# A decoder step whose first two token blocks enter the first projection without their norm

## Chip, cores and metric

One core of a Trainium2 chip. The metric is the device time of one execution in microseconds. Times inside an execution are counted from the start of the span, which runs from the first to the last instruction of the profiled execution.

## What is computed

One layer of a decoder that has two groups of heads: gated linear recurrence (HGRN2) and forgetting attention (FoX). 1024 prompt tokens and 8 x 4 sample tokens, 1024 wide, are normed, projected once, mixed by the two groups, gated, projected back and normed again. The places that matter here:

```python
def rmsnorm(x, w):
    y = xf * lax.rsqrt(jnp.mean(xf * xf, axis=-1, keepdims=True) + NORM_EPS)
    return (y * w.astype(jnp.float32)).astype(x.dtype)

hp = rmsnorm(xp, norm_w[l])
proj = jnp.einsum('btd,dc->btc', h, w_in_l)     # 4104 columns, split among the groups
hq, hf, hi, hgate, fq, fk, fv, ff, fgate = jnp.split(proj, offs, axis=-1)
```

The norm is a factor for each token times a weight for each column. The factor of a token can be taken out of the product: it scales one row of the projection.

## The kernel before

The 1024 prompt tokens are eight blocks of 128 (`tb` 0 to 7), the 32 sample tokens a ninth. A block lies transposed in SBUF, as eight chunks `k` of 128 model columns by 128 tokens (`xts[tb]`). A product of full precision is made of three passes of float32r: a value is split into a rounded part `hi` and the rest `lo`, and `hi*hi`, `hi*lo` and `lo*hi` are summed in PSUM. So all of x is kept as `xhi` and `xlo`, and each weight group as `hi` and `lo`.

The order of the work is written out by hand: every engine runs its instructions in program order, and all DMAs are issued from SP, in order.

- The norm of a block: ScalarE squares it, GpSimd multiplies it by the norm weight `nwT` (L245), VectorE reduces the squares (L249), TensorE sums them over the partitions with a matrix of ones (`norm_r`, in float32, which makes two instructions of one call), ScalarE makes the reciprocal root in two steps (`rstd`, L218 and L219), VectorE multiplies (L265), ScalarE rounds to `xhi` (L269), VectorE subtracts to `xlo` (L273).
- The first projection (`w1`, 512 columns, the recurrence's values): the weights come in four pairs of chunks. `split` makes `hi` (L308 on ScalarE or L310 on VectorE) and `lo` (L311 on VectorE or GpSimd). `proj` takes the block as the stationary side and makes three products of 512 columns for each k. Blocks 0 and 1 use the PSUM tiles `pa` and `pb`; blocks 2 to 7 follow in a loop, with the norm of the coming block between their products. `norm_r(2)` stands in the middle of block 1, `norm_r(3)` after k = 2 of block 2.
- `warm` issues products of ones with ones ahead of the first real work.
- The second projection (`w2`, 520 columns, the gates): `gate_group(tb)` makes two halves of 260 columns, each of 24 products in one of the two PSUM banks `pj`, and VectorE evacuates them (L488, L491, L492). Behind it `silu_mul` runs `Abs`, `Exp`, `Ln` on ScalarE (L336 to L338), one operation on VectorE (L339), `Exp` on ScalarE (L340) and two multiplies on GpSimd (L341, L343). `lower_bound` gives three small steps on `lb` to groups 3 to 5. `slab_split` prepares the first weight slab of the third projection (L448 on ScalarE, L449 on VectorE) after group 2.
- Then come the slabs (`slab`: weights stationary, x moving, all 1056 tokens), the recurrence, the attention, the sample tokens and the output projection. They read `xhi` and `xlo` of all blocks.

`U(i)` names SBUF slot i; a slot is used again when its readers are done. The loads of x wait for their slots, and those queued behind them on SP wait too.

Of the kernel before, what the change touches and what calls it, by code (L numbers as in the profile page):

```python
# [9 lines left out]
F32 = mybir.dt.float32  # L10
# [3 lines left out]
AF = mybir.ActivationFunctionType  # L14
OP = mybir.AluOpType
AX = mybir.AxisListType
# [4 lines left out]
D = 1024  # L21
NB = 8
KB = 8
# [47 lines left out]
def tile_hymba(ctx, tc, x_prompt, x_sample, x_b, x_d, cache_k_t, cache_v, cache_logf_t, state_hgrn, page_table,  # L71
# [10 lines left out]
    V, A, G, PE, SP = nc.vector, nc.scalar, nc.gpsimd, nc.tensor, nc.sync  # L82
# [8 lines left out]
    def f32(ap):  # L91
        return ap.bitcast(F32)

    def mm(out, lhsT, rhs, start, stop):
        PE.matmul(out, lhsT, rhs, start=start, stop=stop, skip_group_check=True)  # L95
# [6 lines left out]
    cst = ctx.enter_context(tc.tile_pool(name="cst", bufs=1))  # L102
# [6 lines left out]
    def U(i, n=TA, dt=F32, a=None):  # L109


        if i not in slots or slots[i].dtype != dt:
            slots[i] = wo["p"].tile([128, 1024], dt, name=f"u{i}") if i >= 100 else up.tile([128, TA], dt, name=f"u{i}")
        t = slots[i][:, :n]
        return t if a is None else t.rearrange("p (a b) -> p a b", a=a)

    def bank(name, n):
        if name not in banks:
            banks[name] = [0, [psum.tile([128, 512], F32, name=f"{name}{i}") for i in range(n)]]
        b = banks[name]  # L120
        b[0] += 1
        return b[1][b[0] % n]

    def ps_pj():
        return bank("pj", 2)

    def ps_s():
        return bank("ps", 3)
# [55 lines left out]
    nwT = cst.tile([128, KB], F32, name="nwT")  # L184
    xts = {}

    def load_x(tb):
        n = 128 if tb < NB else ND
        xts[tb] = U((17, 18, 24, 25, 26, 27)[tb % 6], D, a=KB)[:, :, :n]
        SP.dma_start(xts[tb], (x_b[tb] if tb < NB else x_d).rearrange("p (k t) -> p k t", k=KB))  # L190

    cc = cst.tile([128, K_MK], F32, name="cc")
# [5 lines left out]
    xhi = xp_.tile([128, KB, TA], F32R, name="xhi")  # L198
    xlo = xp_.tile([128, KB, TA], F32R, name="xlo")
# [13 lines left out]
    v = [U(20 + i, 1024, a=2) for i in range(4)]  # L213
# [3 lines left out]
    def rstd(r, ss, n):  # L217
        A.activation(r, ss, AF.Ln, bias=eps[:r.shape[0]], scale=1.0 / n)  # L218
        A.activation(r, r, AF.Exp, scale=-0.5)  # L219


    ones = wk[:, 384:512]
# [5 lines left out]
    def warm(n):  # L228
        for _ in range(n):
            mm(pw[:, :128], ones, ones, True, True)  # L230

    warm(11)

    ss_ = {}

    def norm_sq(tb, parts=1):
        xt, n = xts[tb], xts[tb].shape[-1]
        sq = U(15 + tb % 2, D, a=KB)[:, :, :n]
        o = 512 * (tb % 2)
        s = ss_[tb] = wk[:, o:o + 128 * parts].rearrange("p (a t) -> p a t", a=parts)[:, :, :n]  # L240
        for a in range(parts):
            k = slice(KB // parts * a, KB // parts * (a + 1))
            A.activation(sq[:, k], xt[:, k], AF.Square)
        for k in (slice(0, 4), slice(4, 8)):
            G.tensor_mul(xt[:, k], xt[:, k], nwT[:, k, None].to_broadcast([128, 4, n]))  # L245

        def reduce(a):
            k = slice(KB // parts * a, KB // parts * (a + 1))
            V.tensor_reduce(s[:, a], sq[:, k].rearrange("p k t -> p t k"), axis=AX.X, op=OP.add)  # L249

        return reduce

    def norm_r(tb):
        s, n = ss_[tb], xts[tb].shape[-1]
        p = ps_s()[:, :n]
        m = s.shape[1]
        for a in range(m):
            mm(p, ones, s[:, a], a == 0, a == m - 1)
        o = 512 * (tb % 2) + 256
        rstd(wk[:, o:o + n], p, D)  # L260

    def norm_mul(tb, k):
        xt, n = xts[tb], xts[tb].shape[-1]
        r = wk[:, 512 * (tb % 2) + 256:512 * (tb % 2) + 256 + n]
        V.tensor_mul(xt[:, k], xt[:, k], r[:, None, :].to_broadcast([128, k.stop - k.start, n]))  # L265

    def norm_hi(tb, k):
        xt, n, t0 = xts[tb], xts[tb].shape[-1], tb * 128
        A.activation(xhi[:, k, t0:t0 + n], xt[:, k], AF.Copy)  # L269

    def norm_lo(tb, k):
        xt, n, t0 = xts[tb], xts[tb].shape[-1], tb * 128
        V.tensor_sub(xlo[:, k, t0:t0 + n], xt[:, k], f32(xhi[:, k, t0:t0 + n]))  # L273

    halves = (slice(0, 4), slice(4, 8))

    def norm_a(tb):
        norm_sq(tb)(0)

    def norm_b(tb):  # L280
        norm_r(tb)
        for f in (norm_mul, norm_hi, norm_lo):
            for k in halves:
                f(tb, k)
        if tb == NB:
            V.tensor_copy(xd[:, :, :ND], f32(xhi[:, :, T:]))
            V.tensor_copy(xd[:, :, ND:], f32(xlo[:, :, T:]))
# [57 lines left out]
    w1 = Group(w_1, range(8), (12, 13, 14, 28))  # L345
    w2 = Group(w_2, (8, 9, 10, 11, 28, 29, 4, 5), (13, 14, 12, 13))
    every = slice(0, 512)
    load_x(0)
    SP.dma_start(nwT, norm_w.rearrange("o (k p) -> p (o k)", p=128))
    w1.load(0)  # L350
    load_x(1)
    w1.load(1)
    w1.load(2)
    w1.load(3)
    load_x(2)
    load_x(3)
    red = norm_sq(0, 2)
    red(0)
    red(1)
    w1.split(0, (V, V), (G, G))  # L360
    norm_r(0)
    warm(8)
    red = norm_sq(1)
    thirds = (slice(0, 2), slice(2, 4), slice(4, 8))
    for k in thirds:
        norm_mul(0, k)
        norm_hi(0, k)
    norm_lo(0, thirds[0])
    red(0)
    norm_lo(0, thirds[1])  # L370
    norm_lo(0, thirds[2])
    w1.split(1, (A, A), (V, V))
    load_x(4)
    load_x(5)
    SP.dma_start(cc, consts[:, :K_MK])
    pa, pb = ps_pj(), ps_pj()
    w1.proj(pa, 0, every, (0, 1))
    norm_r(1)
    w1.split(2)
    w1.proj(pa, 0, every, (2, 3))  # L380
    for f in (norm_mul, norm_hi, norm_lo):
        for k in halves:
            f(1, k)
    w1.split(3)
    w1.proj(pa, 0, every, (4, 5))
    red = norm_sq(2)
    w1.proj(pa, 0, every, (6, 7))
    A.activation(v[0][:, 0], pa, AF.Copy)
    red(0)
    w2.load(0)  # L390
    w2.load(1)
    w1.proj(pb, 1, every, (0, 1, 2, 3))
    norm_b(2)
    norm_a(3)
    load_x(6)
    w1.proj(pb, 1, every, (4, 5, 6, 7))
    A.activation(v[0][:, 1], pb, AF.Copy)
    load_x(7)
    load_x(8)
    w2.load(2)  # L400
    SP.dma_start(bf, bcast_row(b_fox_f, FH))
    SP.dma_start(hw, bcast_row(hg_norm_w, HK))
    for tb in range(2, NB):
        if tb < 6:
            norm_a(tb + 2)
        if tb == 7:
            w1.proj_d(vd, every)
        ps = ps_pj()
        w1.proj(ps, tb, every, range(3))
        if tb == 6:  # L410
            norm_b(NB)
        if tb < 7:
            norm_b(tb + 1)
        if tb == 5:
            norm_a(NB)
        w1.proj(ps, tb, every, range(3, 6))
        if tb < 5:
            w2.split(tb - 2)
        if tb == 3:
            w2.load(3)  # L420
        if tb == 7:
            w2.split(3)
        w1.proj(ps, tb, every, range(6, KB))
        A.activation(v[tb // 2][:, tb % 2], ps, AF.Copy)

    mk = U(17, 448, a=7)
    SP.dma_start(mk, consts[:, K_MK:K_N].rearrange("p (l b) -> p l b", l=7))

    v3 = cst.tile([96, 512], F32R, name="v3")
# [13 lines left out]
    def slab_split(i, half):  # L443
        if i < len(slabs):
            raw = U(12, 1024, a=KB)
            h, l = parts[i] = U(13 + i % 2, 1024, F32R, a=KB), U(15 + i % 2, 1024, F32R, a=KB)
            k = slice(4 * half, 4 * half + 4)
            A.activation(h[:, k], raw[:, k], AF.Copy)  # L448
            (V if i < 11 else G).tensor_sub(l[:, k], raw[:, k], f32(h[:, k]))  # L449
# [34 lines left out]
    def gate_group(tb):  # L484
        x = sg[tb // 2][:, tb % 2]
        ps = ps_pj()
        w2.proj(ps[:, :260], tb, slice(0, 260))
        V.tensor_copy(x[:, :260], ps[:, :260])  # L488
        ps = ps_pj()
        w2.proj(ps[:, :260], tb, slice(260, 520))  # L490
        V.tensor_add(zf[:, tb, :], ps[:, 252:260], bf)  # L491
        V.tensor_copy(x[:, 260:], ps[:, :252])  # L492
# [19 lines left out]

    SP.dma_start(lb[:, 0], bass.AP(tensor=hg_lb.tensor, offset=hg_lb.offset, ap=[[1, 128], [128, NH]]))
    lbs = lower_bound()
    for tb in range(NB):
        gate_group(tb)
        if tb == NB - 1:
            log_sigmoid(lf.rearrange("p b h -> p (b h)"), zf.rearrange("p b h -> p (b h)"), 128, 64)
            V.tensor_copy(lfh, lf.rearrange("p b h -> p h b"))
            w2.proj_d(sgd[:, :260], slice(0, 260))  # L520
            w2.proj_d(sgd[:, 260:], slice(260, 520))
        if tb in (3, 4, 5):
            next(lbs)
        silu_mul(sg[tb // 2][:, tb % 2], 128)
        if tb == 0:
            slab_load(0)
        if tb == 2:
            slab_split(0, 0)
            slab_split(0, 1)
            slab_load(1)  # L530
    m8 = U(29, 448).bitcast(U8).rearrange("p (l c b) -> p l c b", l=7, c=4)
    for l in range(len(LEVELS)):
# [910 lines left out]
    for n, (pr, i, q) in enumerate(order):  # L1443
        s = n % 8
# [72 lines left out]
```

## Time and profile before

| | us |
|---|---|
| median of 3 executions | 780.32 (780.12 to 782.49) |
| the profiled execution | 779.85 |
| its span | 778.1 |
| TensorE busy | 740.7 (95%) |
| VectorE busy | 461.8 (59%) |
| ScalarE busy | 356.9 (46%) |
| GpSimd busy | 319.4 (41%) |

The profile's TensorE line over 40 equal slices shows the first slices thinnest, together with the last:

```profile
PE   6999899999999999998999989989999899999996
PEclk8999999999999999999999999999999999999999
```

A digit is the busy share of a slice of 19.5 us in tenths, and in the second line the granted clock in tenths of full speed. Where TensorE is busy all the time, work of the other engines beside it costs nothing; only what TensorE waits for, and stretches at the lower clock, can be shortened.

### The profile page before, as it was taken

How to read it: one execution, taken by the hardware profiler on the slowest of the kernel's cores; microseconds unless marked ns; L12 is line 12 of the kernel's file. 1: busy time of each engine (PE TensorE's matmuls, PEld its weight loads, DVE VectorE, ACT ScalarE, POOL GpSimd, SP SyncE). 2: the span in 40 equal slices, each digit the busy share in tenths (PEclk: the TensorE clock that was granted, in tenths of full speed). 3: DMA queues.
4: the chain of work that ended last, by engine and by line, in shares of the span. 5: the costliest groups of instructions: out<-in, count | busy, mean ns of one | idle time of the engine just before them, and what ended most of it. 6: DMA issues, size and time to landing. Idle time of an engine off the chain costs nothing.

```text
span 778.1 us, 12930 instructions
## 1 busy us (share of the span) xinstructions
PE 740.7 (95%) x4815; PEld 659.7 (85%) x4815; DVE 461.8 (59%) x954; ACT 356.9 (46%) x833; POOL 319.4 (41%) x337
## 2 busy tenths in 40 slices
PE   6999899999999999998999989989999899999996
PEld 5678899998999999997998889979988676577886
DVE  7774324646647665267447844785478776667422
ACT  4562446444242441136546654757466522455312
POOL 4450435373471853535434462536344533332101
PEclk8999999999999999999999999999999999999999
DMA  8411000100221103003101020101111686713521
GB/s 300 134 34 34 1 29 3 60 26 36 84 80 59 55 31 109 29 32 123 44 28 57 29 82 28 57 29 55 55 56 57 210 304 221 258 56 130 190 81 55
DMA packets 28465, 64.99 MB, mean 84 GB/s; under 512 B 6290, under 2 KB 7442, under 8 KB 28402
## 3 DMA queue, kind: packets, MB, share of 16 engines
q1 hardware_dynamic: 28402, 64.16, 23.6%
q8 instruction: 38, 0.62, 0.3%
q14 instruction: 25, 0.20, 0.1%
HBM read 47.27 MB, written 16.88 MB: 82 GB/s over the span
## 4 chain that ended last, share of the span: by engine, by line
PE 71%; DVE 15%; ACT 7%; issue 4%; POOL 1%; DMA 1%; SPq 0%; DVEq 0%; ACTq 0%; POOLq 0%
PE pj L95 52%; PE ps L95 11%; PE po L95 3%; DVE u L856 2%; PE pt L925 2%; DVE u L930 2%; DVE st L895 2%; PE pt L95 1%; ACT u L905 1%; ACT u L929 1%; DMA u<-in_w_dram 1%; DVE u L812 1%; ACT xhi L269 1%; POOL u L311 1%; DVE u L791 1%
## 5 line engine op out<-in xcount | busy, mean ns | idle before, releaser
L95 PE MATMUL pj<-xhi,u 128*128 128x352 f32 x1152 | 315.2, 332 | 0.7 <-DVE u L449 0.5
L95 PEld LDWEIGHTS pj<-xhi,u 128*128 128x128 f32 x1152 | 205.8, 188 | 3.4 <-DVE u L449 0.8
L95 PE MATMUL pj<-xlo,u 128*128 128x352 f32 x576 | 186.2, 323 | 0.0
L95 PE MATMUL ps<-u,u 128*128 128x64 f32 (+7 forms) x952 | 129.7, 272 | 3.4 <-ACT u L905 2.6
L95 PEld LDWEIGHTS ps<-u,u 128*128 128x128 f32 (+2 forms) x952 | 111.8, 178 | 14.4 <-ACT u L905 4.4
L910 POOL TENSOR_SCALAR u<-u,st 128x128 f32<-128x128 f32 (+3 forms) x64 | 48.7, 761 | 153.8 <-DVE st L908 87.7
L95 PEld LDWEIGHTS pj<-xlo,u 128*128 128x128 f32 x576 | 108.6, 189 | 0.7
L95 PE MATMUL pj<-u,xhi 128*128 128x260 f32 (+1 forms) x384 | 90.3, 329 | 4.1 <-DVE u L488 2.2
L905 ACT ACTIVATE u<-ps,st 128x512 f32<-128x512 f32 (+2 forms) x96 | 55.0, 578 | 50.3 <-DVE st L898 21.6
L95 PE MATMUL pj<-h,u 128*128 128x512 f32 (+2 forms) x237 | 74.3, 384 | 0.8 <-DVE h L1046 0.8
L655 POOL TENSOR_TENSOR u<-u,u 128x256 f32<-128x256 f32 (+1 forms) x56 | 40.4, 721 | 84.4 <-PE ps L95 78.8
L95 PEld LDWEIGHTS pj<-u,xhi 128*128 128x128 f32 x384 | 63.9, 191 | 12.2 <-ACT xhi L269 2.5
L930 DVE TENSOR_TENSOR u<-pt,u 128x512 fp32r<-128x512 f32 (+1 forms) x80 | 48.5, 631 | 29.3 <-ACT u L929 28.7
L95 PE MATMUL pj<-u,xlo 128*128 128x260 f32 (+1 forms) x192 | 62.6, 326 | 2.9 <-DVE xlo L273 2.9
L95 PE MATMUL po<-u,u 128*128 128x256 f32 (+1 forms) x320 | 52.3, 287 | 9.3 <-DVE u L930 4.7
L929 ACT ACTIVATE u<-pt 128x512 fp32r<-128x512 f32 (+1 forms) x80 | 41.8, 552 | 41.9 <-PE pt L925 34.2
L895 DVE TENSOR_REDUCE st<-ps 128x1 f32<-128x512 f32 (+2 forms) x96 | 53.3, 556 | 12.4 <-PE ps L95 9.8
L95 PEld LDWEIGHTS po<-u,u 128*128 128x128 f32 x320 | 44.3, 188 | 16.7 <-DVE u L930 7.8
L95 PEld LDWEIGHTS pj<-h,u 128*128 128x128 f32 (+1 forms) x237 | 42.3, 185 | 10.7 <-ACT u L811 1.2
L95 PE MATMUL pj<-u,u 128*128 128x512 f32 (+3 forms) x174 | 46.8, 437 | 2.7 <-ACT u L1213 2.1
L95 PE MATMUL pj<-w,u 128*128 128x512 f32 (+2 forms) x125 | 47.8, 383 | 0.0
L656 POOL TENSOR_TENSOR u<-u,u 128x256 f32<-128x256 f32 (+1 forms) x56 | 43.7, 780 | 0.0
(242 smaller groups left out, 1144.0 us busy)
## 6 DMA issues: line engine op xcount, KB each, us to landing
u<-in_w_s_dram SPq DMA_DIRECT2D x24, 512.0 KB
out_dram<-u SPq DMA_DIRECT2D x12, 512.0 KB
u<-in_x_b_dram SPq DMA_DIRECT2D x8, 512.0 KB
u<-in_cache_k_t_dram SPq DMA_DIRECT2D x16, 256.0 KB
u<-in_cache_v_dram SPq DMA_DIRECT2D x16, 256.0 KB
m_s<-u SPq DMA_DIRECT2D x7, 512.0 KB
u<-m_s SPq DMA_DIRECT2D x14, 256.0 KB
w<-in_w_out_dram SPq DMA_DIRECT2D x12, 256.0 KB
```

What stands on the lines that cost most here:

```text
L95: PE.matmul(out, lhsT, rhs, start=start, stop=stop, skip_group_check=True)
L269: A.activation(xhi[:, k, t0:t0 + n], xt[:, k], AF.Copy)
L311: se[a].tensor_sub(l[:, a], raw[:, a], f32(h[:, a]))
L655: G.tensor_mul(k4[:, :, 0, :], k4[:, :, 0, :], f3[:, eb, 1:2].to_broadcast([128, n, m]))
L656: G.tensor_mul(q4[:, :, 1, :], q4[:, :, 1, :], f3[:, eb, 0:1].to_broadcast([128, n, m]))
L856: V.tensor_sub(K2[o], kf[r, :T], f32(K1[r]))
L895: V.tensor_reduce(st[:, m:m + 1], ps, axis=AX.X, op=OP.min)
L905: A.activation(P[:, s], ps, AF.Exp, scale=-1.0, bias=st[:, lo:lo + 1], accum_out=st[:, 2 + m:3 + m])
L910: G.tensor_scalar(P[:, :e], P[:, :e], st[:, 4:5], 1.0, op0=OP.mult, op1=OP.mult)
L925: PE.transpose(p[:, c:c + 128], probs[n, b][:, j * 128:(j + 1) * 128], ident)
L929: A.activation(ph[:, :w], p[:, :w], AF.Copy)
L930: V.tensor_sub(pl[:, :w], p[:, :w], f32(ph[:, :w]))
```

## The change

Blocks 0 and 1 are multiplied by the norm weight alone (`quick_hi`, `quick_lo`), and their first projection is made of that. The norm factor of each token is found meanwhile: ScalarE squares, TensorE sums with the squares as the stationary side and one column of ones as the moving side (`quick_r`), which gives one factor per partition (`rc`), and the evacuation of `pa` and `pb` applies it as its scale. The second projection and the slabs need the normed x, so `again` makes `xhi` and `xlo` of the two blocks anew, in three steps each, beside the gate groups. The groups of blocks 0 and 1 therefore come last, and x of these blocks keeps its slots 17 and 18; later blocks take others and are loaded later, and the mask tile moves to slot 1. The two halves of the first slab split come after the fourth and the sixth group instead of both after the third. `norm_r(2)` comes after the whole of block 1. `norm_w` is handed over in the layout of its tile, 8 values in a row for each partition, instead of being gathered value by value. The weight pairs 0 and 1 are loaded ahead of block 1, their splits stay on VectorE and ScalarE, the 8 later `warm` calls are gone and the first ones are 14 instead of 11.

```diff
-        xts[tb] = U((17, 18, 24, 25, 26, 27)[tb % 6], D, a=KB)[:, :, :n]
+        xts[tb] = U((17, 18, 24, 25, 26, 27, 24, 25, 26)[tb], D, a=KB)[:, :, :n]
...
-    warm(11)
+    warm(14)
...
+    def quick_hi(tb, k):
+        A.activation(xhi[:, k, tb * 128:tb * 128 + 128], xts[tb][:, k], AF.Copy, scale=nwT[:, k:k + 1])
+    def quick_lo(tb, k):
+        t = slice(tb * 128, tb * 128 + 128)
+        V.scalar_tensor_tensor(xlo[:, k, t], xts[tb][:, k], nwT[:, k:k + 1], f32(xhi[:, k, t]),
+                               op0=OP.mult, op1=OP.subtract)
+    def quick_sq(tb):
+        A.activation(U(15 + tb % 2, D, a=KB), xts[tb], AF.Square)
+    def quick_r(tb):
+        sq, p = U(15 + tb % 2, D, a=KB), ps_s()[:, :1]
+        for k in range(KB):
+            mm(p, sq[:, k], ones[:, :1], k == 0, k == KB - 1)
+        rstd(rc[:, tb:tb + 1], p, D)
+    def again(tb):
+        xt, sq = xts[tb], U(7, D, a=KB)
+        on, s, r = (U(6)[:, i * 128:i * 128 + 128] for i in range(3))
+        if tb == 0:
+            V.memset(on, 1.0)
+        A.activation(sq, xt, AF.Square)
+        for k in halves:
+            G.tensor_mul(xt[:, k], xt[:, k], nwT[:, k, None].to_broadcast([128, 4, 128]))
+        V.tensor_reduce(s, sq.rearrange("p k t -> p t k"), axis=AX.X, op=OP.add)
+        yield
+        p = ps_s()[:, :128]
+        mm(p, on, s, True, True)
+        rstd(r, p, D)
+        for k in halves:
+            V.tensor_mul(xt[:, k], xt[:, k], r[:, None, :].to_broadcast([128, 4, 128]))
+        yield
+        for f in (norm_hi, norm_lo):
+            for k in halves:
+                f(tb, k)
+        yield
...
     load_x(0)
-    SP.dma_start(nwT, norm_w.rearrange("o (k p) -> p (o k)", p=128))
+    SP.dma_start(nwT, norm_w)
     w1.load(0)
+    w1.load(1)
     load_x(1)
-    w1.load(1)
...
+    for k in ks:
+        quick_hi(0, k)
+    for k in ks[:4]:
+        quick_lo(0, k)
+    w1.split(0, (V, V), (V, V))
+    quick_sq(0)
+    for k in ks[4:]:
+        quick_lo(0, k)
     w1.split(1, (A, A), (V, V))
...
+    w1.proj(pa, 0, every, ks[:4])
+    w1.split(2, (A, A), (V, V))
+    w1.proj(pa, 0, every, ks[4:6])
+    w1.split(3, (A, A), (V, V))
+    quick_r(0)
+    for k in ks:
+        quick_hi(1, k)
+    w1.proj(pa, 0, every, ks[6:])
+    for k in ks:
+        quick_lo(1, k)
+    A.activation(v[0][:, 0], pa, AF.Copy, scale=rc[:, 0:1])
     w2.load(0)
     w2.load(1)
+    red = norm_sq(2)
+    quick_sq(1)
+    red(0)
+    w1.proj(pb, 1, every, ks)
     norm_b(2)
+    quick_r(1)
     norm_a(3)
     load_x(6)
+    A.activation(v[0][:, 1], pb, AF.Copy, scale=rc[:, 1:2])
...
+        if tb < 4:
+            load_x(tb + 5)
...
-    mk = U(17, 448, a=7)
+    mk = U(1, 448, a=7)
...
-    for tb in range(NB):
+    anew = [again(0), again(1)]
+    for n, tb in enumerate((2, 3, 4, 5, 6, 7, 0, 1)):
         gate_group(tb)
-        if tb == NB - 1:
+        if n < 6:
+            next(anew[n // 3])
+        if n == NB - 1:
...
-        if tb in (3, 4, 5):
+        if n in (3, 4, 5):
             next(lbs)
         silu_mul(sg[tb // 2][:, tb % 2], 128)
-        if tb == 2:
-            slab_split(0, 0)
-            slab_split(0, 1)
+        if n in (3, 5):
+            slab_split(0, n // 5)
+        if n == 5:
             slab_load(1)
```

## Rows read from the trace of the kernel before

**Rows 1.** Busy time by stretch: us, engines' busy time, granted clock, DMA share, GB/s

```profile
3.50:5.50 2.00, 1.93 (x13) 1.74 (x12) 0.58 (x1) 1.15 (x2) 0.19 (x1) 1.00 0.78 129
11.00:13.50 2.50, 0.00 (x0) 0.00 (x0) 2.50 (x3) 1.42 (x3) 2.37 (x2) 1.00 1.02 419
14.00:22.00 8.00, 7.06 (x19) 4.69 (x17) 7.90 (x11) 3.81 (x9) 1.28 (x1) 0.57 0.77 289
15.00:21.00 6.00, 5.12 (x12) 3.85 (x13) 5.90 (x9) 2.64 (x6) 1.28 (x1) 0.50 0.68 251
```

**Rows 2.** Timeline, TensorE, start: start us, us, instruction, count, idle before

```profile
7.29 1.95 PE L95 MATMUL po<-u 128*128 128x128 f32 x16
...
13.70 0.50 PE L95 MATMUL pj<-u,xlo 128*128 128x512 f32 x1 [2.86 <-DVE xlo L273]
...
25.57 0.39 PE L95 MATMUL pj<-u,xlo 128*128 128x512 f32 x1
...
26.27 0.39 PE L95 MATMUL pj<-u,xlo 128*128 128x512 f32 x1
...
27.21 0.38 PE L95 MATMUL ps<-u 128*128 128x128 f32 x2
27.35 0.71 PE L95 MATMUL pj<-u,xhi 128*128 128x512 f32 x2
...
33.43 0.49 PE L95 MATMUL ps<-u 128*128 128x128 f32 x2 [0.95 <-DVE u L249]
```

**Rows 3.** Timeline, VectorE, the same stretch

```profile
7.44 0.76 DVE L310 CAST u<-u 128x512 fp32r<-128x512 f32 x2 [0.53 <-DMA u<-in_w_dram]
8.30 4.17 DVE L265 TENSOR_TENSOR u<-u,u 128x256 f32<-128x256 f32 x3
...
16.36 1.98 DVE L311 TENSOR_TENSOR u<-u,u 128x512 fp32r<-128x512 f32 x3
...
31.37 3.91 DVE L249 TENSOR_REDUCE u<-u 128x128 f32<-128x1024 f32 x2 [0.26 <-ACT u L243]
```

**Rows 4.** Timeline, ScalarE and GpSimd, the same stretch

```profile
4.26 1.15 ACT L243 ACTIVATE u<-u 128x512 f32<-128x512 f32 x2 [2.23 <-DMA u<-in_x_b_dram]
...
5.31 2.04 POOL L245 TENSOR_TENSOR u<-u,nwT 128x512 f32<-128x512 f32 x2 [4.86 <-DMA nwT<-in_norm_w_dram]
...
27.63 0.37 ACT L218 ACTIVATE u<-ps,eps 128x128 f32<-128x128 f32 x1 [2.42 <-PE ps L95]
...
29.15 1.24 ACT L269 ACTIVATE xhi<-u 128x512 fp32r<-128x512 f32 x2 [0.81 <-DVE u L265]
```

**Rows 5.** Timeline, gate stage, all engines

```profile
89.77 0.63 ACT L336 ACTIVATE u<-u 128x512 f32<-128x512 f32 x1 [2.48 <-DVE u L492]
...
93.20 1.29 POOL L341 TENSOR_TENSOR u<-u,u 128x512 f32<-128x512 f32 x1 [3.18 <-ACT u L340]
...
93.67 1.36 DVE L449 TENSOR_TENSOR u<-u,u 128x512 fp32r<-128x512 f32 x1 [1.22 <-ACT u L448]
...
96.62 0.42 DVE L488 COPY u<-pj 128x260 f32<-128x260 f32 x1
...
97.10 0.51 PE L95 MATMUL pj<-u,xhi 128*128 128x260 f32 x2 [2.19 <-DVE u L488]
...
106.35 0.42 DVE L488 COPY u<-pj 128x260 f32<-128x260 f32 x1
...
112.12 0.42 DVE L488 COPY u<-pj 128x260 f32<-128x260 f32 x1
```

**Rows 6.** Groups by line and shape, 0 to 140 us: busy us, mean ns

```profile
L269 ACT ACTIVATE xhi<-u 128x128 fp32r<-128x128 f32 x2 | 0.5, 305 | 0.4 <-DVE u L265 0.4
L273 DVE TENSOR_TENSOR xlo<-u,xhi 128x128 fp32r<-128x128 f32 x2 | 0.5, 288 | 0.2 <-ACT xhi L269 0.2
```

**Rows 7.** Timeline, TensorE, two products of four moving columns and the next instruction

```profile
181.14 0.28 PE L95 MATMUL ps<-u,u 128*128 128x4 f32 x2
181.28 0.31 PE L682 MATMUL pt<-cc,u 128*128 128x128 f32 x1
```

More of the change, by code (lines that the diff above doesn't have):

```diff
@@ L275, in tile_hymba @@
     halves = (slice(0, 4), slice(4, 8))
+    rc = cst.tile([128, 2], F32, name="rc")
+    def quick_hi(tb, k):
[31 more added lines that the diff above has]
+        yield
     def norm_a(tb):
@@ L356, in tile_hymba @@
     load_x(3)
[L357 to L371, printed above, removed]
+    ks = range(KB)
+    for k in ks:
[6 more added lines that the diff above has]
+        quick_lo(0, k)
     w1.split(1, (A, A), (V, V))
@@ L376, in tile_hymba @@
     pa, pb = ps_pj(), ps_pj()
[L377 to L389, printed above, removed]
+    w1.proj(pa, 0, every, ks[:4])
[9 more added lines that the diff above has]
+    A.activation(v[0][:, 0], pa, AF.Copy, scale=rc[:, 0:1])
     w2.load(0)
     w2.load(1)
-    w1.proj(pb, 1, every, (0, 1, 2, 3))
+    red = norm_sq(2)
+    quick_sq(1)
+    red(0)
+    w1.proj(pb, 1, every, ks)
     norm_b(2)
+    quick_r(1)
     norm_a(3)
     load_x(6)
[L396 to L399, printed above, removed]
+    A.activation(v[0][:, 1], pb, AF.Copy, scale=rc[:, 1:2])
     w2.load(2)
@@ L521, in tile_hymba @@
             w2.proj_d(sgd[:, 260:], slice(260, 520))
-        if tb in (3, 4, 5):
+        if n in (3, 4, 5):
             next(lbs)
         silu_mul(sg[tb // 2][:, tb % 2], 128)
-        if tb == 0:
+        if n == 0:
             slab_load(0)
-        if tb == 2:
-            slab_split(0, 0)
-            slab_split(0, 1)
+        if n in (3, 5):
+            slab_split(0, n // 5)
+        if n == 5:
             slab_load(1)
@@ L1492 @@
         state_hgrn=np.asarray(state_hgrn)[0].transpose(1, 2, 0, 3).reshape(NH, 128, DB * 128),
-        page_table=page_table, norm_w=norm_w,
+        page_table=page_table, norm_w=np.asarray(norm_w).reshape(KB, 128).T,
         w_1=pairs(w[:, C_HI:C_HI + 512]),
```

## Prediction

> **What bounds the kernel now.** I read three views: busy time in chosen stretches, the timeline of each engine over the first 36 us, and the timeline of the gate stage (the second projection). TensorE is the bound almost everywhere, so only its idle or half-clock time can be won. Here is what each view shows.
>
> First the start. From 11.0 to 13.5 us TensorE does nothing, and from 15 to 21 us its granted clock is 0.50, the lower of its two levels (1.2 GHz), though it stood at 1.00 before [rows 1]. The idle time of 2.86 us ends when VectorE has written the first `xlo`, and 0.95 us are lost again at 33.43, where the norm sum of block 3 comes late [rows 2]. VectorE sets the pace: three multiplies by the row norm take 4.17 us [rows 3]. The queue is slowed too: from 3.5 to 5.5 us it is 78% busy and moves 129 GB/s, against 419 later [rows 1]. That is when `nwT` arrives, the load of 1024 separate 4-byte elements, which GpSimd waits for until 5.31 [rows 4].
>
> Then the gate stage. TensorE loses 2.19 us before 97.10, waiting for the evacuation L488, which stands in VectorE's queue behind both halves of the slab split [rows 5].
>
> The change touches both places. What lies behind them waits only on work that shifts with TensorE, so a gain or loss there should reach the end whole. A marker that both kernels have is the norm sum of block 3 (`norm_r(3)`, 33.43 before).
>
> **The start, worked out** (us from the span's start).
>
> Loads: the slow 2 us cost (419-129)/419 x 2 = 1.4 us [rows 1]. `nwT` becomes 128 runs of 32 bytes; the trace has no such load. Bounds: no gain, or all of 1.4. I take all, as it has an eighth of the pieces. The first weight pair lands at 7.44 - 1.4 = 6.05 [rows 3]; at 419 GB/s one of 0.52 MB follows each 1.25 us: pair 1 at 7.3, x1 8.55, pair 2 9.75, pair 3 11.05. Block 0 is there at 4.26 [rows 4] and is not later.
>
> ScalarE: eight `quick_hi` of 128 columns, 0.305 each [rows 6]; a copy with a scale read per partition is not in the trace. The nearest of this width that reads such an operand is L218 at 0.37 [rows 4], so 0.305 to 0.37. I take 0.31, since neighbours overlap: 4.3 to 6.75; at 0.37 the square ends at 8.3, still ahead of VectorE. The square takes 2 x 0.57 at most [rows 4], to 7.8; the copies of pairs 1, 2 and 3 then start when they land.
>
> The Trainium skill (ScalarE: Activation LUTs, "What ACT_TABLE_LOAD costs") gives about 93 ns per operand read per partition and an equal overlap of neighbours; by that one costs about 0.29 (an estimate). L218 agrees with 0.07 more than the plain copy, and the sum would be the same either way.
>
> VectorE: `quick_lo` 0 to 3 follow `quick_hi` and end at 5.9. Split 0: two casts at 0.38 and two subtractions at 0.66 [rows 3], 6.05 to 8.15, with its second subtraction no longer on GpSimd. `quick_lo` 4 to 7: 0.25 each (0.288 with overlap [rows 6]), to 9.15. Splits 1 to 3: six subtractions at 0.66, to 13.1. GpSimd has no work here, so none is slowed as the multiplies were before.
>
> TensorE: one k of a block is three products in 0.70 [rows 2]. k = 0 and 1 run from 6.5 to 8.6, k = 2 waits for its `lo` until 9.8, and k = 5 ends at 12.25. Then `quick_r(0)`: eight calls, two instructions each like the norm sums, with one moving column. The nearest row is that of four columns, two in 0.14 [rows 7], so 1.15; the upper bound is that of the warm-up, 16 in 1.95 [rows 2]. To 13.4; k = 6 and 7 to 14.8; block 1 is 8 x 0.70, to 20.4. Its `quick_hi` waits behind the `rstd` on ScalarE, which waits for `quick_r`; from a norm sum to the end of its `rstd` is 29.15 - 27.21 less a multiply of about 0.7, so at most 1.2 [rows 2, 4], and 13.4 + 1.1 = 14.5, and eight at 0.31 keep ahead of 0.70 per k. The three more warm-up calls end at 6.1, before the first weights. The 8 warm-up calls removed stood beside other work.
>
> Now the price of the new order. `norm_r(2)` stood in the middle of block 1 and now comes behind all of it, at 20.6. From `norm_r(2)` to the first `xhi` took 29.15 + 0.6 - 27.21 = 2.55 before [rows 2, 4], so TensorE, which has only `quick_r(1)` (1.15) for this, idles 1.4. Sum of block 3: ScalarE ends the second `xhi` of block 2 at 23.8 (30.39 - 27.21 = 3.2 later [rows 2, 4]), then the `rstd` of block 1 (one column, taken at 0.5 where 128 columns take 0.37 for the first of its two steps [rows 4]) and the square (1.05), so VectorE reduces from 25.3 to 27.3 (1.95 to 2.0 each [rows 3]). The marker comes at 27.35. Against 33.43 this is 6.1 gained. Bounds: without the load's gain 4.7; with `quick_r` at 1.95, 5.3; with loads 0.5 earlier still, 6.6.
>
> From the marker on the order is as before. `load_x(6)` to `load_x(8)` now wait on SP for blocks 2 to 4 instead of blocks 0 to 2, with `w2.load(2)`, the two small rows and `w2.load(3)` queued behind; each is wanted two blocks later, which is 2 x 8 x 0.70 = 11 us [rows 2]. The mask load waits for a slot of the first weights and is wanted after the gate groups. All nil.
>
> **The gate stage, worked out.** A gate group takes 5.77 (112.12 - 106.35 [rows 5]). The six `again` steps lie on engines with room, but in VectorE's order a group's chain runs: evacuate (0.7 after the group ends), `Abs`, `Exp`, `Ln`, the silu op, `Exp`, then a slab split; L488 of the next group stands behind. The group after that needs its bank. From `Abs` to the end of one split half was 93.67 + 1.36 - 89.77 = 5.26, L488 another 0.35 [rows 5]. A half without company takes 0.66; this one overlapped GpSimd's L341.
>
> Fourth position (n = 3): the reduce (2.0) now stands ahead of the `lb` subtraction, whose result ScalarE needs before `Abs`. So `Abs` starts 2.9 after the group instead of 0.8, L488 ends at 2.9 + 5.26 + 0.35 = 8.5, and TensorE wants it at 5.9: 2.6 lost. The `lb` subtraction may also meet GpSimd's multiplies of block 1: nothing (its operands are tiny) or 0.7 as for the split; I take 0.4. So 3.0. Sixth (n = 5): 0.8 + 5.26 + 0.35 = 6.4 against 5.77: 0.65 lost. At n = 0, 1, 2 and 4 what is added to VectorE (1.3 to 2.0) fits beside the 2.0 of ScalarE's three functions, or delays only work with 1.6 or more to spare. Two added norm sums cost 0.14 each [rows 2]. Stage: 3.0 + 0.65 + 0.3, less the 2.2 of before that goes with the old split = 1.75 lost. Bounds: 0.3 (no more stall than before) to 2.5 (both splits meet GpSimd for 0.4 longer).
>
> The Trainium skill (SBUF — State Buffer, "Who interferes with whom") says that a VectorE operation with two SBUF inputs and a GpSimd operation that reads SBUF exclude each other for the whole instruction, while a reduce never does. The split's 1.36 fits that. By that rule the `lb` subtraction, ready 2.6 after the group, waits for GpSimd's second multiply of block 1, which by the same rows' order ends near 3.1; that is 0.5 and would change the sum by 0.1.
>
> **Sum.** 6.1 - 1.75 = 4.35 gained. On the profiled execution's own 779.85 us (span 778.1 and 1.75 around it) this gives 775.5; that execution lies 0.47 below the median of 780.32, so 776.0 on the median.
>
> **Rivals.**
> - The clock. Before, idle time of 2.86 us came ahead of the fall. Now the longest gaps are 1.0 near 9, 1.4 near 22 and 1.8 near 26, and 2.19 at 97 cost no clock [rows 5]; that speaks against it. Before, the mean of 14 to 22 us is 0.57 [rows 1], so the lower level held for 8 x 0.43/0.5 = 6.9 of them. If it falls once for as long, half of that, 3.4, is lost: 779.4. The skill (TensorE: Matmul & The Clock Gate, "HAM oscillation") warns of just such bursts with waits between; the 2.19 us gap speaks against it here.
> - Slower: the clock falls twice, in the thin stretch from 8 to 13 and again from 21 to 27, where two gaps stand close. That costs 6.9: 782.9. The gain of 4.35 is gone from 8.7 us at the lower level on.
> - The load of `nwT` isn't what slows the queue, and the first weights land at 7.4 as before: 777.4.
> - The gate stage loses only its 0.3, since the two split halves stall no more than the old pair: 774.6.
> - The change doesn't do what it says: VectorE, not the norm, is the bound, and TensorE starts early only to wait at the marker. If the reduce of block 3 ends no earlier than 30, 3.4 are gained: 778.7.
>
> **How the numbers follow.** Forecast 776.0: 0.50. `nwT` 0.12, gate 0.12, marker late 0.09, clock once 0.11, twice 0.06. A measurement tells about 0.3% (2.3 us) from no change. Faster: forecast, `nwT`, gate, and a few hundredths of the others: 0.77. Same: 0.16. Slower: 0.07. The range of 773.6 (both good bounds: 6.6 and 0.3, on the median 774.0, and a little) to 779.6 (clock once) leaves out about 0.15.
>
> **What would show it.** First product near 6.5; clock 1.00 throughout; block 0 ended near 14.8, marker near 27.4; at the sixth gate group's start a wait of TensorE on L488 near 3 us, and none at the fifth. It is wrong if the clock falls, if the first weights still land after 7, or if TensorE waits on other lines in the gate stage.

## The result, and the profile after

The median went from 782.50 us (780.12 to 785.86) to 778.69 us (776.44 to 780.19), ten runs of each; the ratio is 0.9949, with a 95% interval of 0.9931 to 0.9967. So the change gains 0.5%, or 4.0 us of 782.5 (2.6 to 5.4). The forecast was 776.0 within 773.6 to 779.6. The number lies in the range, yet several of its steps did not go as forecast, and a good part of the gain comes from things that no step named.

The profiled execution of after took 778.63 us (span 776.8). First the stretches of [rows 1], with the same columns (us; busy time of TensorE, its weight loads, VectorE, ScalarE, GpSimd; granted clock, DMA share, GB/s):

```profile
3.50:5.50 2.00, 2.00 (x11) 2.00 (x11) 0.64 (x3) 1.07 (x4) 0.00 (x0) 1.00 0.86 239
11.00:13.50 2.50, 2.49 (x7) 1.47 (x6) 2.47 (x5) 1.62 (x3) 0.00 (x0) 0.56 1.03 421
14.00:22.00 8.00, 8.00 (x45) 6.82 (x43) 3.99 (x11) 5.15 (x14) 0.56 (x1) 1.00 0.77 307
```

TensorE now works from 11 to 13.5, where it stood idle, and has the higher level from 14 to 22, where it had the lower one for 6.9 us. But the load stretch is still slow (239 GB/s), and the clock is now low from 11 to 13.5. It fell twice more before 110 us; these are shorter stretches of the same view:

```profile
9.00:10.00 1.00, 0.87 (x3) 0.49 (x3) 0.97 (x3) 0.81 (x2) 0.00 (x0) 0.91 1.01 414
10.00:11.00 1.00, 1.00 (x3) 0.72 (x3) 1.00 (x5) 0.34 (x1) 0.00 (x0) 0.50 1.03 422
13.00:14.00 1.00, 1.00 (x6) 0.79 (x5) 1.00 (x3) 0.97 (x2) 0.00 (x0) 0.89 1.05 422
...
27.00:28.00 1.00, 1.00 (x3) 0.71 (x3) 0.75 (x2) 0.97 (x4) 0.00 (x0) 0.50 0.00 0
...
102.00:102.50 0.50, 0.50 (x4) 0.50 (x4) 0.50 (x2) 0.50 (x1) 0.00 (x0) 0.50 0.00 0
```

The timeline of TensorE at the start (start us, us, instruction, count, idle before), against [rows 2]:

```profile
8.49 0.47 PE L95 MATMUL pj<-u,xhi 128*128 128x512 f32 x1 [1.49 <-DVE u L353]
...
15.12 1.84 PE L95 MATMUL ps<-u,u 128*128 128x1 f32 x16
16.83 0.71 PE L95 MATMUL pj<-u,xhi 128*128 128x512 f32 x2
...
23.85 0.39 PE L95 MATMUL ps<-u 128*128 128x128 f32 x2
24.07 1.84 PE L95 MATMUL ps<-u,u 128*128 128x1 f32 x16
26.48 0.91 PE L95 MATMUL pj<-u,xhi 128*128 128x512 f32 x2 [0.56 <-ACT xhi L269]
...
30.43 0.49 PE L95 MATMUL ps<-u 128*128 128x128 f32 x2
```

The first product starts at 8.49 (forecast 6.5), each `quick_r` holds TensorE for 1.71 us (15.12 to 16.83), and the marker, the norm sum of block 3, comes at 30.43 instead of 33.43. So the start gains 3.0 us. The timelines of VectorE and ScalarE say why it starts late ([rows 3, 4]):

```profile
4.43 2.45 ACT L282 ACTIVATE xhi<-u,nwT 128x128 fp32r<-128x128 f32 x8 [2.40 <-DMA nwT<-in_norm_w_dram]
...
7.92 0.43 DVE L353 CAST u<-u 128x512 fp32r<-128x512 f32 x1 [1.82 <-DMA u<-in_w_dram]
...
28.39 3.89 DVE L249 TENSOR_REDUCE u<-u 128x128 f32<-128x1024 f32 x2 [0.64 <-ACT u L243]
```

The `xhi` of block 0 is under way at 4.43, but the first weights land at 7.92, later even than the 7.44 of before. Now the gate stage, all engines, fourth group ([rows 5]; L307 is the added reduce, L306 GpSimd's added multiplies, L511 the `lb` subtraction, L379 the `Abs`, L487 the split, L526 the evacuation that was L488):

```profile
92.46 2.05 DVE L307 TENSOR_REDUCE u<-u 128x128 f32<-128x1024 f32 x1
92.96 2.04 POOL L306 TENSOR_TENSOR u<-u,nwT 128x512 f32<-128x512 f32 x2
94.40 0.61 DVE L511 TENSOR_TENSOR lb<-lb 128x4 f32<-128x4 f32 x1
95.05 0.20 ACT L512 ACTIVATE lb<-lb 128x4 f32<-128x4 f32 x1 [3.87 <-DVE lb L511]
95.16 0.62 ACT L379 ACTIVATE u<-u 128x512 f32<-128x512 f32 x1
...
99.05 1.33 DVE L487 TENSOR_TENSOR u<-u,u 128x512 fp32r<-128x512 f32 x1 [1.22 <-ACT u L486]
100.31 0.42 DVE L526 COPY u<-pj 128x260 f32<-128x260 f32 x1
100.78 0.51 PE L95 MATMUL pj<-u,xhi 128*128 128x260 f32 x2 [2.79 <-DVE u L526]
...
114.69 0.48 PE L95 MATMUL pj<-u,xhi 128*128 128x260 f32 x2 [0.61 <-DVE u L526]
```

Read it downward: the reduce ends at 94.5, the subtraction behind it only at 95.0, `Abs` starts at 95.16, the split ends at 100.4, and TensorE, which could have gone on at 98.0, starts at 100.78. One microsecond later the clock is at the lower level for 3.4 us. The end of the stage is the first product that reads `xd`, in the timeline of before and then of after:

```profile
120.27 3.97 PE L95 MATMUL pj<-u,xd 128*64 128x260 f32 x32
```

```profile
120.53 4.00 PE L95 MATMUL pj<-u,xd 128*64 128x260 f32 x32
```

In this execution everything that the start gained is lost again by here: 3.0 gained by the marker, then 3.26 lost, of which the waits are 2.79 + 0.61 - 2.19 = 1.2, two more norm sums 0.3, and the clock 3.4 x 0.5 = 1.7. At 120 us the two profiled executions are level. Two more executions of the same order, without the fall at 9.8, are ahead there: the runs n1 and p2 below reach this product at 119.28 and 118.60. So the gain in the medians can't be read from these two traces alone, and the experiments had to find it.

### The profile page after: what moved, and what is told of

The parts are those of the page before. It is cut to its first block, busy times and chain, and to the rows that moved or that the text cites. A ratio compares the mean times of both kernels' runs of the same rounds, so it can differ in the third digit from the quotient of the medians.

```text
span 776.8 us, 13010 instructions
## 1 busy us (share of the span) xinstructions
PE 744.2 (96%) x4835; PEld 665.3 (86%) x4835; DVE 466.2 (60%) x972; ACT 363.8 (47%) x853; POOL 314.5 (40%) x333
## 4 chain that ended last, share of the span: by engine, by line
PE 74%; DVE 13%; ACT 8%; issue 3%; DMA 1%; POOL 1%; SPq 0%; DVEq 0%; ACTq 0%; POOLq 0%
PE pj L95 54%; PE ps L95 11%; PE po L95 3%; PE pt L966 2%; DVE u L897 2%; DVE u L971 2%; DVE st L936 1%; PE pt L95 1%; ACT u L970 1%; ACT u L946 1%; DMA u<-in_w_dram 1%; ACT xhi L269 1%; DVE u L832 1%; DVE u L853 1%; DVE u L998 1%
## 5 line engine op out<-in xcount | busy, mean ns | idle before, releaser
L95 PE MATMUL ps<-u,u 128*128 128x64 f32 (+6 forms) x984 | 133.3, 271 | 3.5 <-ACT u L946 2.6
L95 PEld LDWEIGHTS ps<-u,u 128*128 128x128 f32 (+2 forms) x984 | 115.6, 178 | 14.4 <-ACT u L946 4.4
L95 PE MATMUL pj<-u,xhi 128*128 128x260 f32 (+1 forms) x384 | 91.9, 333 | 5.9 <-DVE u L526 3.4
L696 POOL TENSOR_TENSOR u<-u,u 128x256 f32<-128x256 f32 (+1 forms) x56 | 41.9, 748 | 83.6 <-PE ps L95 78.1
L966 PE MATMUL pt<-cc,u 128*128 128x128 f32 x288 | 42.2, 274 | 0.6 <-ACT u L826 0.5
```

The costliest lines, as they stand in the source:

```text
L696: G.tensor_mul(k4[:, :, 0, :], k4[:, :, 0, :], f3[:, eb, 1:2].to_broadcast([128, n, m]))
L966: PE.transpose(p[:, c:c + 128], probs[n, b][:, j * 128:(j + 1) * 128], ident)
```

## Experiments

Each ratio is taken to runs of the kernel before on the same chip, made together with it (their medians were 782.5 to 784.2). A gain in us below is (1 - ratio) x 782.5. "Marker" is the norm sum of block 3, "end of gate" the first product that reads `xd`.

**The kernel before once more** (`b1_before`, unchanged).

> The kernel before, profiled once more. Theory: its time varies from execution to execution with the places at which the granted clock falls, and the first profiled execution (779.85) had few falls. Then this profile shows the same instruction times up to the first difference in the clock, and any time beyond 779.9 goes with stretches at 0.50 which the first profile lacks, the stall near 95 us (2.2 us) being the likeliest place. Rival: the executions differ in their waits or DMAs, and the granted clock is the same in both profiles.

It took 782.67 us, marker at 33.46 and end of gate at 120.36: the same to 0.1 us. The 2.8 us by which it is longer than the execution profiled first lie behind: its clock fell near 430 and 451, and for twice as long near 618. The first two cost 2.5 us together, read from two products around them, in the first profile and then in this one (36.76 and 39.23 apart):

```profile
422.55 1.03 PE L95 MATMUL po<-u,u 128*128 128x256 f32 x8
...
459.31 1.04 PE L95 MATMUL po<-u,u 128*128 128x256 f32 x8
```

```profile
422.70 1.03 PE L95 MATMUL po<-u,u 128*128 128x256 f32 x8
...
461.93 1.04 PE L95 MATMUL po<-u,u 128*128 128x256 f32 x8
```

So the 779.85 us on which the prediction's sum stands is one of the fastest executions of before, 2.65 below the median of ten.

**The split between the two evacuations, in before** (`s1_before_split_between`): the cause of the 2.19 us wait taken away, nothing else.

```
-    def gate_group(tb):
+    def gate_group(tb, half=None):
...
+        if half is not None:
+            slab_split(0, half)
+            if half:
+                slab_load(1)
...
-        gate_group(tb)
+        gate_group(tb, {3: 0, 4: 1}.get(tb))
...
-        if tb == 2:
-            slab_split(0, 0)
-            slab_split(0, 1)
-            slab_load(1)
```

> The kernel before, with only that edit: the halves of its slab split between the two evacuations of gate groups 4 and 5. Theory: its wait of 2.2 us at 95 us goes, and where the clock falls behind that wait in some executions, 1.7 us more: ratio 0.995 to 0.997, less wide a spread. Rival: the wait comes back at a later evacuation: ratio 1.000.

779.06 us, ratio 0.9952 (0.9938 to 0.9966), end of gate at 118.14. The 2.2 us are gone there, and this one edit gains as much as the whole change: 3.8 us in the medians (2.7 to 4.9), 1.6 more than the wait. A fall of the clock behind the wait, as `p1_before_tile8` below shows one, would be worth that; how many executions of before have it isn't known.

**The same in after** (`g1_split_between`): the halves in the gate groups n = 4 and 6, by the same lines in `gate_group`, and the `lb` step ahead of `again`.

```
...
-        gate_group(tb)
+        gate_group(tb, {4: 0, 6: 1}.get(n))
+        if n in (3, 4, 5):
+            next(lbs)
         if n < 6:
             next(anew[n // 3])
...
-        if n in (3, 4, 5):
-            next(lbs)
...
-        if n in (3, 5):
-            slab_split(0, n // 5)
-        if n == 5:
-            slab_load(1)
```

> The changed kernel, with the two halves of the slab split put between the two evacuations of gate groups 5 and 7 instead of in front of the first evacuation, and the three small lb steps put ahead of the again steps. Theory: TensorE's waits on L526 in the gate stage (2.8 and 0.6 us) come from the order on VectorE alone, and the stretch at half clock behind the first of them (3.4 us long, 1.7 us lost) from the wait. Both go: 5 us less than the changed kernel, ratio to before 0.988 to 0.990. Rival: the six again steps have filled VectorE, and the waits only move to another evacuation: ratio as the changed kernel's, 0.995.

772.28 us, ratio 0.9864 (0.9841 to 0.9886): 6.7 us better than the change. The waits of TensorE from 0 to 140 us (total us, times, longest), first in after, then here:

```profile
PE pj L95 <- DVE u L526: 3.4, 2, 2.8
PE pj L95 <- DVE u L353: 1.5, 1, 1.5
```

```profile
PE ps L95 <- DVE u L249: 1.3, 1, 1.3
...
PE pj L95 <- DVE u L354: 0.9, 2, 0.7
...
PE pj L95 <- DVE u L487: 0.4, 1, 0.4
```

The waits on the evacuation are gone, and with them the fall of the clock near 100: the first one in this trace comes after 440 us. The stage takes 84.68 us from the marker to its end (after 90.10), that is 3.4 of waits, 1.7 of clock and 0.3 of the rest.

**Without the `again` steps** (`g2_no_again`; it leaves out the norm of the first two blocks behind the first projection).

```
-        if n < 6:
-            next(anew[n // 3])
```

> The changed kernel without the again steps: x of the first two blocks stays without its norm in the second projection and the slabs, so that part of the computation is left out. It measures what the again steps cost. Theory: the reduce of the second again stands ahead of lb and lengthens the wait behind the fourth group from 0.6 to 2.8 us; without the steps each split half costs 0.6, the clock doesn't fall there, and two norm sums of 0.14 go: 4.3 us less than the changed kernel, ratio to before 0.989 to 0.991. Rival: the split halves alone make the wait: at most 1 us less than the changed kernel, ratio 0.994.

773.6 us, ratio 0.9880 (0.9858 to 0.9902). Two waits on the evacuation are left, 1.6 us together, and no fall near 100. So what `again` puts into VectorE's order turns these into the 2.8 us wait, as forecast. With the split moved instead (g1), the `again` steps stay in and the kernel is no slower than here.

**The old layout of the norm weight, in after** (`n1_nwt_strided`), **and no load of it at all** (`n2_no_nwt_load`, which leaves out the scaling by the norm weight).

```
-    SP.dma_start(nwT, norm_w)
+    SP.dma_start(nwT, norm_w.rearrange("o (k p) -> p (o k)", p=128))
```

```
-    SP.dma_start(nwT, norm_w)
+    V.memset(nwT, 1.0)
```

> The changed kernel with the old load of the norm weight, 1024 pieces of 4 bytes. The prediction's theory: these pieces slow the queue, and with them back the first weights land 1.4 us later than in the changed kernel and the marker, the norm sum of block 3, comes later by as much: ratio to before 0.9965 to 0.997. Rival, which the changed kernel's trace favours (its first weights landed at 7.9, not at 6.05): the queue has a slow stretch near 5 us whatever the pieces are, and nothing changes but block 0's first operation, which waits for the norm weight some tenths longer: 0.995.

> The changed kernel without any load of the norm weight: the tile is set to one, so the scaling by the norm weight is left out. If the load in either layout is what slows the queue between 4 and 6.5 us, that stretch moves 400 GB/s and more and the first weights land near 6.1. If not, 115 to 300 GB/s remain there and they land at 7.4 to 7.9.

With 1024 pieces of 4 bytes: 778.46 us, ratio 0.9938 (0.9915 to 0.9962), first cast of the weights at 7.55, marker at 29.41. The layout is worth nothing that can be told in the time. Without the load: 775.82 us, ratio 0.9903 (0.9875 to 0.9932), marker at 27.96. Busy time by stretch, and two rows of the timeline, without the load:

```profile
3.50:5.50 2.00, 2.00 (x18) 2.00 (x18) 0.57 (x2) 1.00 (x4) 0.00 (x0) 1.00 1.00 391
```

```profile
6.08 0.42 DVE L353 CAST u<-u 128x512 fp32r<-128x512 f32 x1
...
6.64 0.47 PE L95 MATMUL pj<-u,xhi 128*128 128x512 f32 x1 [0.77 <-ACT xhi L282]
```

So the load does hold the first weights up, by some 1.5 us at the cast (7.55 - 6.08), and 128 runs of 32 bytes hold the cast up as much as 1024 pieces: from 6.88 to 7.92 in the six kernels that have them (after, g1, g2, h1, w1, p2; 7.40 in the mean), and from 7.44 to 7.71 in the five with 1024 pieces. But it isn't the whole queue that is slow. The trace records 16 landings for each load, and the cast waits for the last (7.90 in after, the cast at 7.92). Of the first weights, twelve have landed by 6.6 to 7.2 us with 1024 pieces, by 5.4 to 6.1 with 128 runs and by 5.58 without the load; the last lands at 7.4 to 7.7, at 6.85 to 7.90 and at 5.64. So the new layout does free most of the landings, by about 1 us, and VectorE waits for the few that it doesn't. Without the load VectorE isn't ready before 6.08, so that this agrees with the 6.05 forecast for the landing is chance.

**Eight long rows, turned on TensorE** (`r1_nwt_rows` in after; `r2_early_nwt_rows` in `h1_block2_early`, below). The eight rows hold 128 weights each and a row of an identity; six of the 14 warm-up calls now follow the transpose.

```
-    SP.dma_start(nwT, norm_w)
+    nwr = U(7, 128 + KB)[:KB]
+    SP.dma_start(nwr, norm_w)
+    nwp = ps_s()[:, :KB]
+    PE.transpose(nwp, nwr[:, :128], nwr[:, 128:])
+    warm(6)
+    V.tensor_copy(nwT, nwp)
```

> The kernel after, with the norm weight loaded as 8 runs of 544 bytes (its 8 rows of 128, and an 8x8 identity behind them) and turned on TensorE between the first 8 and the last 6 warm-up calls. Without the load the first weights landed at 6.08 and the marker came at 27.96; with 128 runs of 32 bytes at 7.92 and 30.43 (of which about 1.6 was the clock). Theory (the number of small pieces slows the queue): no stretch below 300 GB/s between 3.5 and 6 us, first weights at 6.1 to 6.3, marker near 28, total 775.8, as without the load. Rival (any transfer ahead of the weights that is small slows it): weights at 7.3 or later, marker near 29.5, total 778.5.

> The kernel with the split halves between the evacuations and block 2's norm ahead of block 1's square (marker at 26.92, 770.05 us), with the norm weight loaded as 8 runs of 544 bytes and turned on TensorE. Theory: first weights at 6.1 to 6.3 instead of 7.26, marker at 25.6 to 25.9, total 768.8. Rival (the start then waits on VectorE or on x): marker stays at 26.5 to 27, total 770.

777.89 us, ratio 0.9916 (0.9901 to 0.9931), and 769.73 us, ratio 0.9819 (0.9805 to 0.9832). The stretch of the load in the one and in the other:

```profile
3.50:5.50 2.00, 2.00 (x10) 1.75 (x10) 0.17 (x1) 0.18 (x1) 0.00 (x0) 1.00 0.86 286
```

```profile
3.50:5.50 2.00, 2.00 (x12) 1.75 (x12) 0.17 (x1) 0.23 (x1) 0.00 (x0) 1.00 1.00 324
```

The first cast starts at 7.89 and at 6.85, and the markers come at 29.77 and 26.28. In `r1_nwt_rows` fifteen of the 16 landings are there by 6.63 and the last at 7.86; in `r2_early_nwt_rows` all are there by 5.58, as without any load, and there VectorE itself, busy with `quick_lo` until then, comes to the cast only at 6.85. So with eight rows a late landing came in one execution and not in the other, and where it stayed away the start waits on VectorE, as the second expectation's rival says. The first kernel is 0.3% better than after by its ratio, with intervals that touch, and the second level with `h1_block2_early`. Which landings come late, and why, stays open.

**Twice the warm-up** (`w1_warm28`): `warm(28)` for `warm(14)` in after.

> The changed kernel with 28 calls of the warm-up products instead of 14, which at 0.12 us an instruction keep TensorE busy up to about 8.9 us, past the first weights' arrival. Theory: the fall of the clock at 9.9 us comes from the idle time before it; without it no stretch at 0.50 before 14 us and, at the marker, 0.7 to 1.0 us less, in those executions that had the fall: ratio to before 0.993 to 0.995. Rival: the thin work from 8.5 to 13 us brings the fall, or the warm-up only delays the first products: 0.995 to 0.997.

779.1 us, ratio 0.9941 (0.9918 to 0.9963): no difference. No fall came at the start here, but none came at 9.8 in n1, n2, g1, g2, h1, r1, r2 or p2 either, and none of these has a longer warm-up than after. Of the ten traces with the new start, after's alone has it: the fall at 9.8 is a matter of the execution.

**Block 2's norm ahead of block 1's square, on top of g1** (`h1_block2_early`): `quick_sq` gets slots of its own (22, 23), and the order becomes

```
     w1.split(3, (A, A), (V, V))
+    norm_sq(2)(0)
     quick_r(0)
...
-    red = norm_sq(2)
     quick_sq(1)
-    red(0)
-    w1.proj(pb, 1, every, ks)
+    w1.proj(pb, 1, every, ks[:4])
     norm_b(2)
-    quick_r(1)
     norm_a(3)
+    w1.proj(pb, 1, every, ks[4:])
+    quick_r(1)
```

> The kernel with the slab split between the evacuations, and in the start the squares and the reduce of block 2 placed ahead of the token sums of block 0 (in slots of their own), the norm of block 2 in the middle of block 1 again and the squares of block 3 behind it. Theory: the two waits of the start that the new order made (0.6 on xhi, 1.3 on the reduce of block 3) are only a matter of order; the marker comes at 27 instead of 29.4 us: 2 us less than the kernel without this edit, ratio to before 0.983 to 0.985. Rival: VectorE and ScalarE are full there and the waits come back in block 2 or 3: ratio 0.986.

770.05 us, ratio 0.9830 (0.9805 to 0.9854), marker at 26.92 (29.45 in g1). Of these 2.5 us, 0.3 are weights that came earlier (first cast at 7.26, in g1 at 7.59); 2.2 are the price of the order in which `norm_r(2)` stands behind all of block 1. The kernel beats before and after.

**The places of the tiles** (`p1_before_tile8`, `p2_after_tile64`). One thing was left: read instruction by instruction, before, b1 and s1 keep a constant distance from 155 to 355 us, while after and every kernel made from it gains steadily there, with TensorE busy and the same instructions. After allocates one tile more, `rc`, of 8 bytes per partition, and what is allocated behind it moves. So before got this tile, unused, and after got a larger one:

```
     zf = cst.tile([128, NB, FH], F32, name="zf")
+    cst.tile([128, 2], F32, name="rc")
```

```
-    rc = cst.tile([128, 2], F32, name="rc")
+    rc = cst.tile([128, 16], F32, name="rc")[:, :2]
```

> The kernel before with nothing but the one added tile of after, rc, two floats (8 bytes) per partition, here never used. Read instruction by instruction, the traces of before, of before run again and of before with the split between run level from 155 to 355 us, while that of after and those of all kernels made from it gain steadily there (0.35 us from 155 to 340, about 1.7 to 610) with TensorE busy throughout and the same instructions. Theory (the tile moves every tile allocated behind it by 8 bytes, and the products read their operands a little faster): the steady gain appears here too, ratio 0.998. Rival (it is the changed program, not the places of its tiles): level with before, ratio 1.000.

> The kernel after with rc in a tile of 64 bytes per partition instead of 8. Theory (places): the steady gain from 155 to 610 us is gone if 64 bytes leave the places as good or bad as they were before: 1.7 us longer, 780.4. Rival (not the places): as after, 778.7, with the steady gain.

Before with the unused tile: 780.37 us (780.12 to 780.61, seven runs) against 784.03 (781.57 to 786.09, twelve), ratio 0.9957 (0.9941 to 0.9973), or 3.4 us. After with 64 bytes: 779.23 us, ratio 0.9943 (0.9924 to 0.9962), as after. How much is gained steadily can be read from two products that every trace has, the one of [rows 7] and one near 600 us. Before (the first of the two is 181.14 [rows 7]):

```profile
603.11 0.49 PE L925 MATMUL pt<-cc,u 128*128 128x128 f32 x3
```

With the unused tile:

```profile
182.70 0.28 PE L95 MATMUL ps<-u,u 128*128 128x4 f32 x2
...
603.57 0.49 PE L926 MATMUL pt<-cc,u 128*128 128x128 f32 x3
```

In r1, which like before has no fall of the clock between them:

```profile
181.79 0.28 PE L95 MATMUL ps<-u,u 128*128 128x4 f32 x2
...
601.83 0.49 PE L971 MATMUL pt<-cc,u 128*128 128x128 f32 x3
```

From one to the other: before 421.97 us, r1 420.04, r2 420.14, p2 420.66; with the unused tile 420.87, or 1.10 less than before. On the way there the clock fell near 357 with the unused tile, but this cost nothing: from a product ahead of it to one behind it, before takes 39.00 and this kernel 38.90.

```profile
340.46 0.72 PE L95 MATMUL pt<-u,K 96*128 96x512 f32 x2
...
379.46 1.07 PE L95 MATMUL po<-u,u 128*128 128x256 f32 x8
```

```profile
341.67 0.71 PE L95 MATMUL pt<-u,K 96*128 96x512 f32 x2
...
380.57 1.07 PE L95 MATMUL po<-u,u 128*128 128x256 f32 x8
```

So the unused tile gains 1.1 us of 422 steadily, or 0.26%, mostly in steps too small to be seen one by one. The kernels made from after gain up to 1.9. In r1, 0.6 of that lies in two short waits, at 418 and 428 (the second is 0.76 us there, 1.08 in before and 1.07 with the unused tile), which the tile alone doesn't shorten. The rest of the 3.4 is likely, for the most part, the clock. The execution profiled with the unused tile is the median one and has no fall near 430 or 451, where b1 loses 2.5 by two; the first profile of before has none there either. The runs of before spread over 4.5 us and those with the tile over 0.5, but one trace doesn't show that the tile keeps these falls away. That an unused tile, with the same instructions, makes the kernel faster is shown; which tile has to stand where is open, since 64 bytes did what 8 did. After without any added tile was not tried.

## Why the prediction was right in its number and wrong in its steps

**The load of `nwT`: wrong.** The step was "I take all, as it has an eighth of the pieces". The size was about right (without the load the marker comes 1.45 earlier than in n1), but the new layout wins none of it at the cast (n1). What failed is the reading of the 129 GB/s as a queue slowed as a whole: with 128 runs most landings do come earlier, and the cast waits for the last one. This was a rival with a chance of 0.12. It is 7.92 - 6.05 = 1.9 of what the marker misses, 0.5 of it the luck of this execution, as the six kernels with this load start the cast at 7.40 in the mean.

**ScalarE's copies: right.** Eight in 2.45 us, 0.306 each, forecast 0.31. VectorE's six subtractions took 3.88, or 0.65 each, as forecast, and only began later.

**`quick_r`: mis-sized.** 1.71 us for 16 instructions, 0.107 each, where 1.15 was taken from the products with four columns; the upper bound of 1.95, from the warm-up, held it. 0.56 lost.

**The clock at the start: wrong.** "Clock 1.00 throughout" failed. It fell at 9.8, and from the first product to `quick_r(0)` took 6.63 us (15.12 - 8.49) against 6.0 in n1, so 0.63 was lost. The fall at 26.9 cost nothing. From `norm_r(2)` to the marker after took 6.58 (30.43 - 23.85), and n1, without that fall, 6.56 (29.41 - 22.85): there TensorE waits 1.32 us for the norm sum of block 3 instead. In this stretch VectorE's reduce set the time in both.

**The new order of block 2: right.** 20.6 to 27.35 was forecast for this stretch, 6.75 us; it took 6.58. So the start's 6.1 became 6.1 - 1.9 - 0.56 - 0.63 = 3.0 with the clock, and 33.43 - 29.41 = 4.0 without its fall and with weights at 7.55: below the lower bound of 4.7, since `nwT` and `quick_r` failed together.

**The gate stage's waits: right.** 2.79 and 0.61 at the places named, forecast 3.0 and 0.65; the `lb` subtraction was held up from 0.146 to 0.61 us, by 0.46, forecast 0.4. The rule weighed there (the Trainium skill, SBUF — State Buffer, "Who interferes with whom") agrees with the trace: the subtraction of 4 columns, two inputs from SBUF, ends at 95.01, when GpSimd's second multiply ends at 95.00. The reduce beside the first multiply took 2.05 us, not much more than the 1.93 of a reduce of before beside which GpSimd does nothing:

```profile
13.57 1.93 DVE L249 TENSOR_REDUCE u<-u 128x128 f32<-128x1024 f32 x1
```

**The clock in the gate stage: wrong.** "2.19 at 97 cost no clock" was used as a reason that a longer wait would cost none either. All six traces with the wait of 2.7 to 2.8 us there (after, n1, n2, w1, r1, p2) show a fall that begins in the wait or up to 1.3 us behind it and lasts 3.4 us, or twice that in r1 and w1. The five in which the wait is gone or at most 1.0 us (s1, g1, g2, h1, r2) show none. So 2.19 was no safe ground: the wait is there three times, in before and b1 without a fall and in p1 with one. The page cited for this rival (the Trainium skill, TensorE: Matmul & The Clock Gate, "HAM oscillation") shows a kernel in which every short burst of products is followed by a wait for DMA longer than itself. Here the trace agrees in the fall but not in the pattern: one wait of 2.7 to 2.8 us in work that is dense on both sides has it.

**"The order is as before" behind the marker: wrong in one point.** No step looked at where tiles lie. The diff holds a new tile of 8 bytes, and this alone is worth 3.4 us in the medians of before, 1.1 of them a steady gain that the traces show.

**The sum.** In place of 6.1 - 1.75 = 4.35, one reckoning of the parts measured is: start 4.0 less 0.3 for the two sums, waits in the gate stage -1.2, clock behind them -1.7, together 0.8; with 3.4 for the tile 4.2, where 4.0 (2.6 to 5.4) were measured. The same parts give for g1 3.7 + 3.4 + 3.8 (s1) = 10.9, measured 10.6. But this isn't the only one. The tile's part was measured on before alone, and if executions of before often have the fall behind their wait of 2.19, as p1 does and as the 3.8 of s1 suggest, the change doesn't add the 1.7; then its mechanism is worth 2.5, and 1.5 are left for the tile and the falls near 430 and 451. The runs don't tell the two apart. By either, the forecast's mechanism is worth 0.8 to 2.5 us where 4.35 were forecast, and something that it did not name makes up for the rest. That the forecast gain is so near the measured one is luck. The step from the profiled execution to the median was mis-sized too: 0.47 us by three runs, 2.65 by ten, so that 4.35 off the median of ten would have been 778.2.

## What to carry to other kernels

Price a wait by what stands ahead of the producer in its engine's order, as was done here, and then add the clock that may fall behind it: moving the split between the two evacuations was worth 3.8 us in s1 and, with the `lb` step, 6.7 in g1, where the whole start of the change gained 3.0 to 4.0. When a change allocates a tile, run the old kernel with that tile unused before crediting the new order with the gain. And take the distance between a profiled execution and the median from ten runs, not from three.

## What the runs showed of the hardware

- An unused tile of 8 bytes per partition made the kernel 0.43% faster (0.27 to 0.59), and its runs spread over 0.5 us instead of 4.5.
- The same wait of TensorE brought a fall of the granted clock to the lower level (1.2 GHz) in some executions and not in others. All fourteen traces have a wait of 2.08 us between 347 and 358, one of 1.7 between 438 and 451 and one of 2.1 between 605 and 619; within the wait or up to 2.7 us behind it the clock fell in 7, in 8 and in all 14 of them.
- A stretch at the lower level lasted 3.4 us or twice that, and cost from nothing (near 357) to half its length (1.7 us, in the gate stage of after).
- A load of 4 KB ahead of the first weights held up the last of their 16 landings from 5.64 us to 7.4 to 7.7 with 1024 pieces and to 6.85 to 7.90 with 128, but the twelfth from 5.58 only to 6.6 to 7.2 and to 5.4 to 6.1.
- Products with one moving column (`quick_r`) came 0.107 us apart, no faster than those with four columns (two in 0.14 [rows 7]).
